# Part of the first feed-forward product by seven products of quarters in place of eight, and new planner prices for TensorE

## Chip, core and metric

One core of a Trainium2 chip runs the whole program in one launch. The metric is the device time of that launch in microseconds (us); lower is better.

## What is computed

Two layers of an encoder on 512 tokens of 1024 features. Each layer has a mixing half (one combined projection, a causal pooling mixer, sparse attention with an indexer, an output projection) and a feed-forward half. The change touches the feed-forward half alone:

```python
h = rms_norm(x, g_pre_ffn[l])
f = jnp.square(jax.nn.relu(h @ w_ff1[l])) @ w_ff2[l]
x = x + rms_norm(f, g_post_ffn[l])
```

`w_ff1` is 1024 x 4096 and `w_ff2` 4096 x 1024, all in float32.

## The kernel before

**Three passes.** TensorE works on float32r, which holds fewer digits than float32. So each float32 operand is split into a high part (a rounded copy) and a low part (operand minus high part), and each product is three matmuls: high x high, high x low, low x high (`PASSES`, line 700; `mm3`, line 702).

**Weights.** `WeightStream` (line 385) brings all weights in the order of their use. A load of 256 rows x 512 columns lands in one of two raw buffers (`wraw`); `_split` (line 445) turns each 128 rows of it into a chunk `ws` of two parts, one `copy` (high) and one `tt` subtraction (low). Eight chunks can be held (`NWS`, line 36): chunk n+8 can be split only when the last matmul on chunk n is done.

**Feed-forward.** `h`, transposed and split, lies in `A` (128 x 2 parts x 8 row blocks x 512 tokens), written by `pre_norm` (line 662) for one tile of 128 tokens at a time. The first product is made in eight blocks of 512 columns. Block 0 runs in two halves of 256 tokens, so that it can start when two token tiles are normed (banks `pf`). Blocks 1 to 7 run on all 512 tokens: 8 row blocks x 4 column tiles x 3 passes = 96 matmuls of 128 x 512, into four PSUM banks `pg`. `evac_f` (line 996) takes each bank through ReLU, square and the split into parts (tiles `fr`, then `f1h`/`f1l` or `f`). After two blocks comes their share of the second product (`ff2`): two halves of 8 chunks, 96 matmuls of 512 each, added to `facc`. Two blocks with their `ff2` are called a group here; there are four groups in a layer.

**Order.** `Planner` (line 82) records all instructions and issues them in the order of a list schedule, from a price for each instruction (`cost`, line 356) and from dependencies. What several engines can do, it assigns itself: `tt` is VectorE or GpSimd, `copy` is ScalarE or VectorE. Every engine then executes its own list in order. Since all instructions are issued from one helper, the profile puts them all on line 349; they are told apart by tile names.

Of the kernel before, what the change touches and what calls it, by code (L numbers as in the profile page):

```python
# [38 lines left out]
OUT_ORDER = (0, 1, 2, 3, 4, 5, 6, 7)  # L39
REPLACED = -3.0e38  # L40
# [41 lines left out]
class Planner:  # L82
    """Takes the instructions down in program order, finds what each depends on from the tiles that it
    reads and writes, and issues them in the order of a list schedule over the engines: of the
    instructions that an engine could start, the one with the longest chain of work behind it."""
# [141 lines left out]
    def sweep(self, key, pred, succ, late, fixed=None):  # L227
        """A list schedule. With ``fixed``, the ways are given and time runs backward."""
# [107 lines left out]
class _Recorder:  # L336
# [19 lines left out]
    def cost(self, method, args, kw, out, reads):  # L356
# [8 lines left out]
        if self.name == "pe":  # L365
            if method == "transpose":
                return 56 if args[1].dtype == F32R else 109
            return max(n / 2.4 + 2.5, 107 if free(args[1]) > 64 else 56)
# [16 lines left out]
class WeightStream:  # L385
    """Chunks of weights in the order of their use: loaded, split into two float32r parts, and held
    in a ring until their last use."""

    def __init__(self, copy, tt, sp, raw_pool, ws_pool):
        self.copy, self.tt, self.sp = copy, tt, sp  # L390
        self.raw_pool, self.ws_pool = raw_pool, ws_pool
# [4 lines left out]
        self.raw = {}  # L396

# [11 lines left out]
    def add_paired(self, src, r0, nrows, c0, ncols):  # L409
        """Chunks of 256 rows: rows r and r + 128 side by side."""  # L410
        ids = []
        for r in range(r0, r0 + nrows, 4 * P):
            k = len(self.loads)
            self.loads.append((src, r, -2, c0, ncols))
            for j in range(2):
                ids.append(len(self.chunks))
                self.chunks.append((k, j, 2 * ncols))
        return ids
# [8 lines left out]

    def _load(self):
        if self.n_load >= len(self.loads):
            return  # L430
        src, r, n, c0, ncols = self.loads[self.n_load]
        t = self.raw_pool.tile([P, 2, WMAX], F32, name="wraw")
# [12 lines left out]
    def _split(self):  # L445
# [6 lines left out]
        raw = self.raw[k][:, j, :n]  # L452
        w = self.ws_pool.tile([P, 2, WMAX], F32R, name="ws")
        self.tiles.append(w)
        self.n_split += 1
        self.copy(w[:, 0, :n], raw)
        self.tt(w[:, 1, :n], raw, w[:, 0, :n].bitcast(F32), OP.subtract)
        if j == abs(self.loads[k][2]) - 1:
            self._load()
# [10 lines left out]
def hymba_trunk(ctx: ExitStack, tc: tile.TileContext, x, positions, g_pre_mix, w_in, w_pool,  # L470
# [23 lines left out]
    wkp = ring("wkp", 1)  # L494
    tiny = ring("tiny", 4)
# [11 lines left out]
    def t2(name):  # L507
        return t2p.tile([P, WMAX], F32, name=name, tag="t2")
# [22 lines left out]
    def tt(out, a, b, op, first="dve"):  # L531
        """an elementwise instruction on SBUF, on VectorE or GpSimd"""
# [12 lines left out]
    ws = WeightStream(copy, tt, sp, rawp, wsp)  # L545
    plan = []
    for l in range(DEPTH):
# [14 lines left out]
        for g in range(4):  # L562
            for b in (2 * g, 2 * g + 1):
                p["ff1", b] = ws.add(w_ff1[l], 0, D, 512 * b, 512)
# [21 lines left out]
    identf = cst.tile([P, P], F32, name="identf")  # L586
    make_identity(nc, identf)
    ident = cst.tile([P, P], F32R, name="ident")
    dve.tensor_copy(ident, identf)
# [72 lines left out]
    def pre_norm(t, gain):  # L662
        """A[:, :, :, tile t] = the two parts of (RMSNorm(x[t]) * gain) transposed."""
# [10 lines left out]
        for hf in range(2):  # L674
# [3 lines left out]
            for j in range(4):  # L678
# [30 lines left out]
    def rope(row, t, heads):  # L709
        """in place on the first 16 of each head's 64 columns."""  # L710
# [8 lines left out]
    def heads_stacked(dst_hl, row, heads):  # L719
        """dst[128, heads, 2, 64]: the two parts of each head side by side."""  # L720
# [4 lines left out]
    def heads_doubled(dst, row, heads):  # L725
        """dst[128, 2, heads, 2, 64]: either part of each head, twice side by side."""
# [4 lines left out]
    def transposed(dst, srcs):  # L731
        """dst [128, n, 128] <- transposes of n blocks of [128, 128] in float32r."""
# [14 lines left out]
    for l in range(DEPTH):  # L747
# [4 lines left out]
        wp = cst.tile([P, 2, 4, P], F32R, name=f"wp{l}", tag="wp")  # L752
        wpr = t2("wpr")[:, :512]
        sp.dma_start(wpr.rearrange("p (g n) -> p g n", g=4), w_pool[l].rearrange("g p n -> p g n"))
        act.activation(wp[:, 0], wpr.rearrange("p (g n) -> p g n", g=4), AF.Copy)
        pool.tensor_tensor(wp[:, 1], wpr.rearrange("p (g n) -> p g n", g=4), wp[:, 0].bitcast(F32),
                           op=OP.subtract)

        # indexer projection, logits and scores
        work, iqS = {}, {}  # L760
        score = {}
        for t in range(NT):
# [26 lines left out]
            acc = wkp.tile([P, n], F32, name=f"sc{t}", tag=f"sc{t}")  # L789
# [16 lines left out]
        def select(t):  # L806
            n = P * (t + 1)
            acc = score[t]
            b = wkp.tile([P, n], F32, name=f"bias{t}", tag=f"bias{t}")
            bias[t] = b  # L810
            if n > TOPK:
                m8 = small(8, f"m8{t}")
# [50 lines left out]
        # attention  # L863
# [48 lines left out]
        def pooling_mixer():  # L912
# [12 lines left out]
            for g in POOL_PAIRS[0] + POOL_PAIRS[1]:  # L925
# [18 lines left out]
                mm3(ps, lambda a: wp[:, a, g, :], lambda b: dh[:, b], True, True)  # L944
# [6 lines left out]
        load_gain(("pre_ffn", l), g_pre_ffn, l)  # L951

        def out_pair(pair):
# [12 lines left out]
            for i, t in enumerate(tt):  # L966
                post_norm(t, banks[i], gains["post_mix", l])
                pre_norm(t, gains["pre_ffn", l])
# [13 lines left out]
        # feed-forward  # L982
        facc = None
        for g in range(4):
            f1 = []
            for bi in range(2):
# [41 lines left out]
            for hf in range(2):  # L1028
# [20 lines left out]
                for t in range(NT):  # L1049
                    if g == 0:  # L1050
                        copy(facc[:, t, cs], banks[t])
                    else:
                        dve.tensor_tensor(facc[:, t, cs], banks[t], facc[:, t, cs], op=OP.add)
        for t in range(NT):
# [30 lines left out]
```

## Time and profile before

| what | value |
|---|---|
| median of 3 runs | 1223.35 us (1222.4 to 1226.63) |
| profiled execution, first to last instruction | 1222.7 us |
| TensorE (PE) busy | 1178.5 us, 96% |
| VectorE (DVE) busy | 777.1 us, 64% |
| GpSimd (POOL) busy | 668.5 us, 55% |
| ScalarE (ACT) busy | 358.5 us, 29% |
| granted TensorE clock, mean | 0.996 of 2.4 GHz |

The page gives no other time for the profiled execution than its span, which lies inside the range of the runs. Busy time counts an instruction from its start to its end, and includes what it waits for inside. The kernel moves 115 MB through its queues, 94 GB/s in the mean.

### The profile page before, as it was taken

How to read it: one execution, taken by the hardware profiler on the slowest of the kernel's cores; microseconds unless marked ns; L12 is line 12 of the kernel's file. 1: busy time of each engine (PE TensorE's matmuls, PEld its weight loads, DVE VectorE, ACT ScalarE, POOL GpSimd, SP SyncE). 2: the span in 40 equal slices, each digit the busy share in tenths (PEclk: the TensorE clock that was granted, in tenths of full speed). 3: DMA queues.
4: the chain of work that ended last, by engine and by line, in shares of the span. 5: the costliest groups of instructions: out<-in, count | busy, mean ns of one | idle time of the engine just before them, and what ended most of it. 6: DMA issues, size and time to landing. Idle time of an engine off the chain costs nothing.

```text
span 1222.7 us, 16265 instructions
## 1 busy us (share of the span) xinstructions
PE 1178.5 (96%) x5880; PEld 978.3 (80%) x5880; DVE 777.1 (64%) x1620; ACT 358.5 (29%) x840; POOL 668.5 (55%) x628
## 2 busy tenths in 40 slices
PE   5999999999999999999989999999999999999996
PEld 5987878788888888888887878787888888888885
DVE  8899999875216335245779999998632353343344
ACT  5444677540010000000354367675201000000011
POOL 4145331358659659558334543314785695684782
PEclk9999999999999999999999999999999999999999
DMA  7222222433332322332322222234234223323221
GB/s 242 70 56 67 69 69 88 138 105 121 106 101 69 121 86 71 119 93 90 113 70 69 69 69 69 71 104 138 86 104 121 87 83 107 104 86 104 87 87 69
DMA packets 62160, 115.41 MB, mean 94 GB/s; under 512 B 5248, under 2 KB 10368, under 8 KB 62080
## 3 DMA queue, kind: packets, MB, share of 16 engines
q1 hardware_dynamic: 62080, 114.38, 29.9%
q8 instruction: 46, 0.75, 0.3%
q14 instruction: 34, 0.28, 0.1%
HBM read 112.27 MB, written 2.10 MB: 94 GB/s over the span
## 4 chain that ended last, share of the span: by engine, by line
PE 68%; DVE 23%; issue 5%; POOL 1%; DMA 1%; ACT 0%; DVEq 0%; SPq 0%; POOLq 0%; ACTq 0%
PE pg L349 58%; DVE ws L349 4%; DVE bias L349 3%; PE pi L349 2%; DVE m L349 2%; PE pf L349 2%; DVE mx L349 2%; DVE sc L349 2%; DVE x L349 1%; DVE s L349 1%; DVE A L349 1%; DVE h L349 1%; DVE pT L349 1%; PE lg L349 1%; PE pool L349 1%
## 5 line engine op out<-in xcount | busy, mean ns | idle before, releaser
L349 POOL TENSOR_TENSOR ws<-wraw,ws 128x512 fp32r<-128x512 f32 x296 | 397.6, 1350 | 278.0 <-DVE ws L349 233.3
L349 DVE CAST ws<-wraw 128x512 fp32r<-128x512 f32 (+1 forms) x317 | 195.3, 624 | 337.1 <-PE pg L349 247.4
L349 PE MATMUL pg<-A,ws 128*128 128x512 f32 x1344 | 313.9, 395 | 0.0
L349 PEld LDWEIGHTS pg<-A,ws 128*128 128x128 f32 x1344 | 252.3, 188 | 60.0
L349 PE MATMUL pg<-ws,A 128*128 128x512 f32 x864 | 226.3, 400 | 1.9 <-DVE pn L349 1.6
L349 PE MATMUL pg<-ws,f 128*128 128x512 f32 x768 | 187.0, 394 | 0.0
L349 PEld LDWEIGHTS pg<-ws,A 128*128 128x128 f32 x864 | 156.9, 188 | 33.5 <-DVE pn L349 2.5
L349 PEld LDWEIGHTS pg<-ws,f 128*128 128x128 f32 x768 | 144.1, 188 | 33.6
L349 ACT ACTIVATE fr<-pg 128x512 f32<-128x512 f32 x49 | 27.9, 598 | 475.9 <-PE pg L349 475.1
L349 PE MATMUL pg<-ws,f1h 128*128 128x512 f32 x512 | 149.5, 394 | 0.0
L349 PEld LDWEIGHTS pg<-ws,f1h 128*128 128x128 f32 x512 | 96.1, 188 | 22.5
L349 POOL TENSOR_TENSOR rstd<-rstd,neg_half 128x1 f32<-128x1 f32 x32 | 25.9, 809 | 119.5 <-DVE rstd L349 114.9
L349 PE MATMUL pg<-ws,f1l 128*128 128x512 f32 x256 | 89.1, 393 | 0.0
L349 DVE TENSOR_TENSOR ws<-wraw,ws 128x512 fp32r<-128x512 f32 (+1 forms) x104 | 79.0, 772 | 0.9 <-ACT ws L349 0.5
L349 POOL TENSOR_TENSOR fr<-fr 128x512 f32<-128x512 f32 (+1 forms) x70 | 71.3, 1033 | 12.8 <-ACT fr L349 11.8
L349 ACT ACTIVATE s<-s,st 128x384 f32<-128x384 f32 (+3 forms) x96 | 54.0, 568 | 36.0 <-DVE st L349 32.5
L349 PE MATMUL pi<-ws,A 128*128 128x292 f32 x384 | 60.7, 305 | 2.2 <-DVE ws L349 1.8
L349 ACT ACTIVATE ws<-wraw 128x512 fp32r<-128x512 f32 (+1 forms) x83 | 51.9, 632 | 30.1 <-PE pg L349 19.8
L349 PE MATMUL pool<-A,ws 128*128 128x512 f32 x192 | 58.7, 407 | 0.0
L349 PEld LDWEIGHTS pg<-ws,f1l 128*128 128x128 f32 x256 | 48.1, 188 | 11.2
L349 PEld LDWEIGHTS pi<-ws,A 128*128 128x128 f32 x384 | 53.4, 190 | 3.7 <-DVE ws L349 2.4
L349 DVE CAST f1h<-fr 128x512 fp32r<-128x512 f32 (+1 forms) x40 | 39.2, 997 | 19.0 <-POOL fr L349 19.0
(154 smaller groups left out, 1493.7 us busy)
## 6 DMA issues: line engine op xcount, KB each, us to landing
wraw<-in_w_ff_dram SPq DMA_DIRECT2D x128, 512.0 KB, 3.7
wraw<-in_w_out_dram SPq DMA_DIRECT2D x32, 512.0 KB, 3.6
wraw<-in_w_in_dram SPq DMA_DIRECT2D x24, 512.0 KB, 3.6
wraw<-in_w_in_dram SPq DMA_DIRECT2D x8, 584.0 KB, 4.1
wraw<-in_w_in_dram SPq DMA_DIRECT2D x16, 256.0 KB, 3.0
x<-in_x_dram SPq DMA_DIRECT2D x4, 512.0 KB, 6.3
out_dram<-x SPq DMA_DIRECT2D x8, 256.0 KB, 2.0
gain<-in_g_pre_mix_dram SPq DMA_DIRECT2D x2, 512.0 KB, 4.7
```

What stands on the lines that cost most here:

```text
L349: lambda: getattr(self.real, method)(*args, **kw))
```

## The change

Blocks 1 to 7 of the first product are made by a scheme of seven products. `h` (its transpose) and the 1024 x 512 weights of a block are cut into quarters: two halves of the 1024 rows, two halves of the columns, two halves of the tokens. Each of the seven products is one combination of weight quarters (names `11`, `12`, `S2`, `S1`, `S3`, `S4`, `22`) with one combination of token quarters (from `A`, or the new `T1` to `T4`): 4 row blocks x 2 column tiles x 3 passes = 24 matmuls of 128 x 256. So a block is 7 x 24 = 168 matmuls of 256 columns.

Of a block's weights, each load of 4 row blocks ("unit", tile `uraw`, 1 MB in two DMAs) is made into 7 chunks instead of 4, each split into two parts as before; four additions per unit, partly in place, make the combinations (`usum` holds one). The two units of a block lie in the two buffers `t8`, so that a unit of the next block is loaded only after the last chunk (`22`) of the same half of this one is split. `T1` to `T4` are made once per layer from an unsplit copy `hraw` of `h`. Three of the seven results are kept in SBUF (`p1`, `u2`, `p5`) and three evacuations begin with an addition.

TensorE's price goes from n / 2.4 + 2.5 to n / 2.25 + 4.5 ns for n columns. To make room, several tiles share buffers with others; block 0, the second product and the mixing half compute what they did.

```diff
-            return max(n / 2.4 + 2.5, 107 if free(args[1]) > 64 else 56)
+            return max(4.5 + n / 2.25, 111 if free(args[1]) > 64 else 60)
...
+    COMBINATIONS = ("11", "12", "S2", "S1", "S3", "S4", "22")
...
+    def add_unit(self, src, r0, c0):
...
+        for cp in range(2):
+            self.loads.append((src, r0 + 2 * cp * P, "unit", c0, 512))
+        ids = {}
+        for name in self.COMBINATIONS:
+            ids[name] = []
+            for cp in range(2):
+                ids[name].append(len(self.chunks))
+                self.chunks.append((k + cp, name, 512))
...
+        if name in ("11", "12"):
+            halves(quarter(0, int(name[1]) - 1))
+        elif name == "S2":
+            s1 = v(self.sum_pool.tile([P, 512], F32, name="usum", tag="usum"))
+            self.sums[k] = s1
+            self.tt(s1, quarter(1, 0), quarter(1, 1), OP.add)
+            self.tt(quarter(1, 0), quarter(0, 0), quarter(1, 0), OP.subtract)
+            self.tt(quarter(0, 0), s1, quarter(0, 0), OP.subtract)
+            self.tt(quarter(0, 1), quarter(0, 1), quarter(0, 0), OP.subtract)
+            halves(quarter(0, 0))
...
+            if raw is not None:
+                copy(raw[:, hf, 1 - t // 2, :, (t % 2) * P:(t % 2 + 1) * P], pv)
...
+        tt(total["T1"], hraw[:, 0, 1], hraw[:, 0, 0], OP.subtract)
...
+        for name in ("T2", "T1", "T3", "T4"):
+            copy(T[name][0], total[name])
+            tt(T[name][1], total[name], T[name][0].bitcast(F32), OP.subtract)
...
+            def product(bank, name, other, new=False):
+                for cp in range(2):
+                    w = ws.get(ids[name][cp])
+                    for j in range(2):
+                        for c in range(2):
+                            for i, (a, b) in enumerate(PASSES):
+                                pe.matmul(bank[:, 256 * j:256 * j + 256],
+                                          w[:, a, 256 * c + P * j:256 * c + P * j + P],
+                                          T[other][b][:, 2 * cp + c],
...
+            product(one, "11", "11", True)
+            p1 = kept(one, "p1")
+            product(two, "12", "21", True)
+            evac(0, LATER, two, p1)
+            product(one, "S2", "T2")
+            u2 = kept(one, "u2")
+            two = pg("two")
+            product(two, "S1", "T1", True)
+            p5 = kept(two, "p5")
+            product(one, "S3", "T3")
+            evac(1, SOONER, one, p5)
+            product(two, "S4", "22")
+            evac(0, SOONER, two, u2)
+            product(one, "22", "T4")
+            evac(1, LATER, one)
...
-                    banks = [pg() for _ in range(4)]
-                    for kc in range(KC):
-                        w = ws.get(ids[kc])
-                        for j in range(4):
-                            mm3(banks[j], lambda a: w[:, a, j * P:(j + 1) * P], lambda b: A[:, b, kc, :],
-                                kc == 0, kc == KC - 1)
-                        ws.done()
-                    for j in range(4):
-                        evac_f(j, banks[j], slice(0, S))
+                    unit_products(ids, f)
```

How the planner now orders two engines in the second group of the first layer (blocks 2 and 3). GpSimd before, from the subtractions that make the low parts of weight chunks (`ws`), some of them of blocks 2 and 3, on to the first evacuations of block 2 (`fr` squares, `f1l` low parts):

```order
L349 TENSOR_TENSOR ws<-wraw,ws 128x512 x23
L349 TENSOR_TENSOR fr<-fr 128x512 x2
L349 TENSOR_TENSOR ws<-wraw,ws 128x512
L349 TENSOR_TENSOR f1l<-fr,f1h 128x512
L349 TENSOR_TENSOR ws<-wraw,ws 128x512
```

GpSimd now, at the same place (`usum` and `uraw` as outputs are the additions that make the combinations):

```order
L350 TENSOR_TENSOR usum<-uraw 128x512 x2
L350 TENSOR_TENSOR uraw<-uraw 128x2x256
L350 TENSOR_TENSOR ws<-wraw,ws 128x512
L350 TENSOR_TENSOR uraw<-uraw 128x2x256
L350 TENSOR_TENSOR ws<-wraw,ws 128x512 x2
L350 TENSOR_TENSOR ws<-uraw,ws 128x512
L350 TENSOR_TENSOR uraw<-usum,uraw 128x2x256
L350 TENSOR_TENSOR ws<-uraw,ws 128x512
L350 TENSOR_TENSOR uraw<-usum,uraw 128x2x256
L350 TENSOR_TENSOR ws<-uraw,ws 128x512
```

The additions stand between the subtractions, which were alone here before. From the first chunk of block 2 to the first of block 4, GpSimd's list now has 57 rows: 49 tensor-tensor instructions on 512 elements and 8 squares.

VectorE now, in blocks 2 and 3, around the place where block 3's weights replace block 2's (`fr<-two,p` and `fr<-one,p` are additions that read PSUM):

```order
L350 TENSOR_TENSOR fr<-one,p_805 128x512
L350 TENSOR_SCALAR fr<-fr 128x512
L350 TENSOR_TENSOR uraw<-uraw 128x2x256
L350 CAST ws<-uraw 128x512
L350 TENSOR_TENSOR uraw<-usum,uraw 128x2x256
L350 CAST ws<-uraw 128x512
L350 TENSOR_TENSOR usum<-uraw 128x512
L350 CAST ws<-uraw 128x512 x2
L350 TENSOR_TENSOR uraw<-uraw 128x2x256
L350 TENSOR_TENSOR ws<-uraw,ws 128x512
L350 TENSOR_TENSOR uraw<-usum,uraw 128x2x256
```

VectorE now makes part of the additions and subtractions too. From the first chunk of block 2 to the first of block 4 its list has 87 rows: 50 casts, 19 tensor-tensor instructions on SBUF operands alone, 6 ReLUs on SBUF and 12 instructions that read PSUM. ScalarE's has 10 rows in the same stretch, 8 of them on PSUM.

## Rows read from the trace of the kernel before

**Rows 1.** The page: busy time, share of the span and instructions of each engine.
```profile
PE 1178.5 (96%) x5880; PEld 978.3 (80%) x5880; DVE 777.1 (64%) x1620; ACT 358.5 (29%) x840; POOL 668.5 (55%) x628
```
**Rows 2.** The chain that ended last, in order of time: start us, us, what.
```profile
265.26 5.67 PE pf L349 x48
270.94 5.95 PE pf L349 x48
276.89 328.79 PE pg L349 x1416
...
879.53 325.66 PE pg L349 x1404
```
**Rows 3.** Windows, feed-forward of layer 1: us, busy us (x instructions) of engines, clock, DMA.
```profile
core 0: us, PE busy (x) PEld busy (x) DVE busy (x) ACT busy (x) POOL busy (x), PEclk, DMA share, GB/s
367.00:456.00 89.00, 89.00 (x386) 71.97 (x385) 37.59 (x48) 4.53 (x8) 61.58 (x49) 1.00 0.30 95
277.00:606.00 329.00, 329.00 (x1421) 266.12 (x1420) 141.62 (x198) 25.56 (x49) 224.15 (x177) 1.00 0.31 98
```
**Rows 4.** Timeline, 250 to 281 us, TensorE: start us, us, instruction, count [idle before].
```profile
265.02 11.87 PE L349 MATMUL pf<-A,ws 128*128 128x256 f32 x96
```
**Rows 5.** Instructions on tile ws, 367 to 456 us: duration ns min/median/max, first and last start.
```profile
L349 POOL TENSOR_TENSOR ws<-wraw,ws x32: 1282/1292/1480, 367.6 to 453.5; 128x512 fp32r<-128x512 f32 x32
L349 DVE CAST ws<-wraw x32: 408/429/1544, 369.2 to 455.3; 128x512 fp32r<-128x512 f32 x32
```
**Rows 6.** Timeline, 387 to 404 us, GpSimd.
```profile
393.61 2.91 POOL L349 TENSOR_TENSOR ws<-wraw,ws 128x512 fp32r<-128x512 f32 x2
396.48 1.04 POOL L349 TENSOR_TENSOR fr<-fr 128x512 f32<-128x512 f32 x1
397.48 1.29 POOL L349 TENSOR_TENSOR f<-fr,f 128x512 fp32r<-128x512 f32 x1
399.13 1.29 POOL L349 TENSOR_TENSOR f<-fr,f 128x512 fp32r<-128x512 f32 x1 [0.36 <-DVE f L349]
400.38 4.15 POOL L349 TENSOR_TENSOR ws<-wraw,ws 128x512 fp32r<-128x512 f32 x3
```
**Rows 7.** The same timeline, VectorE.
```profile
392.42 2.94 DVE L349 CAST ws<-wraw 128x512 fp32r<-128x512 f32 x2
...
400.40 2.97 DVE L349 CAST ws<-wraw 128x512 fp32r<-128x512 f32 x2 [1.35 <-DMA wraw<-in_w_ff_dram]
```
**Rows 8.** Timeline, 565 to 584 us, GpSimd and VectorE where VectorE adds or subtracts.
```profile
568.72 1.49 POOL L349 TENSOR_TENSOR fr<-fr 128x512 f32<-128x512 f32 x1
...
567.91 2.84 DVE L349 TENSOR_TENSOR fr<-fr 128x512 f32<-128x512 f32 x2
570.67 0.75 DVE L349 CAST f<-fr 128x512 fp32r<-128x512 f32 x2
571.35 0.68 DVE L349 TENSOR_TENSOR f<-fr,f 128x512 fp32r<-128x512 f32 x1
```
**Rows 9.** Timeline, 408 to 413 us, VectorE adding PSUM to SBUF while GpSimd works.
```profile
410.24 1.87 DVE L349 TENSOR_TENSOR facc<-pg,facc 128x512 f32<-128x512 f32 x3
...
410.45 1.29 POOL L349 TENSOR_TENSOR ws<-wraw,ws 128x512 fp32r<-128x512 f32 x1 [0.41 <-PE pg L349]
```
**Rows 10.** DMA issues: count, KB each, median us from issue to landing.
```profile
wraw<-in_w_ff_dram SPq DMA_DIRECT2D x128, 512.0 KB, 3.7
```
**Rows 11.** Waits of TensorE, the three longest: us in total, times, longest us.
```profile
PE hT L349 <- DVE h L349: 13.0, 4, 9.4
PE tr L349 <- DVE ihl L349: 3.6, 2, 3.0
PE po L349 <- DVE early L349: 3.5, 3, 1.9
```
**Rows 12.** Groups by form, whole span, of ScalarE's casts of weights.
```profile
L349 ACT ACTIVATE ws<-wraw 128x512 fp32r<-128x512 f32 x76 | 47.1, 627 | 28.6 <-PE pg L349 18.3 <-DMA wraw<-in_w_out_dram 8.3 <-PE pi L349 0.6
```

More of the change, by code (lines that the diff above doesn't have):

```diff
@@ L396, in __init__ @@
         self.raw = {}
+        self.sums = {}
+        self.in_use = {"raw": 0, "unit": 0}
+        self.units_allowed = False
     def add(self, src, r0, nrows, c0, ncols):
@@ L426, in start, with _ahead @@
             self._split()
+    def _ahead(self):
+        while self.n_load < len(self.loads):
+            unit = self.loads[self.n_load][2] == "unit"
+            kind = "unit" if unit else "raw"
+            if self.in_use[kind] >= (2 if unit else NRAW) or unit and not self.units_allowed:
+                return
+            self._load()
     def _load(self):
@@ L431, in _load @@
         src, r, n, c0, ncols = self.loads[self.n_load]
+        if n == "unit":
+            self.in_use["unit"] += 1
+            t = self.unit_pool.tile([P, 2048], F32, name="uraw", tag="t8").rearrange(
+                "p (k c n) -> p k c n", k=2, c=2)
+            self.raw[self.n_load] = t
+            self.n_load += 1
+            for k in range(2):
+                self.sp.dma_start(t[:, k], src[r + 4 * k * P:r + (4 * k + 2) * P, c0:c0 + ncols].rearrange(
+                    "(c p) n -> p c n", p=P))
+            return
+        self.in_use["raw"] += 1
         t = self.raw_pool.tile([P, 2, WMAX], F32, name="wraw")
@@ L455, in _split @@
         self.n_split += 1
+        if isinstance(j, str):
+            self._combine(k, j, w)
+            return
+        raw = self.raw[k][:, j, :n]
         self.copy(w[:, 0, :n], raw)
@@ L458, in _split, with _combine, quarter, v @@
         if j == abs(self.loads[k][2]) - 1:
-            self._load()
+            self.in_use["raw"] -= 1
+            self._ahead()
+    def _combine(self, k, name, w):
+        raw = self.raw[k]
+        def quarter(i, j):
+            return raw[:, j, :, 256 * i:256 * i + 256]
+        def v(ap):
+            return ap.rearrange("p (c n) -> p c n", c=2)
+        high, low = v(w[:, 0, :512]), v(w[:, 1, :512])
+        def halves(value):
+            self.copy(high, value)
+            self.tt(low, value, high.bitcast(F32), OP.subtract)
+        if name in ("11", "12"):
[8 more added lines that the diff above has]
+            halves(quarter(0, 0))
+        elif name == "S1":
+            halves(self.sums[k])
+        elif name == "S3":
+            halves(quarter(1, 0))
+        elif name == "S4":
+            halves(quarter(0, 1))
+        else:
+            halves(quarter(1, 1))
+            self.in_use["unit"] -= 1
+            self._ahead()
     def get(self, i):
@@ L563, in hymba_trunk @@
             for b in (2 * g, 2 * g + 1):
-                p["ff1", b] = ws.add(w_ff1[l], 0, D, 512 * b, 512)
+                p["ff1", b] = ws.add_unit(w_ff1[l], 0, 512 * b) if b else ws.add(w_ff1[l], 0, D, 512 * b, 512)
             for hf in range(2):
@@ L951, in hymba_trunk @@
         load_gain(("pre_ffn", l), g_pre_ffn, l)
+        hraw = c1p.tile([P, 2, 2, 4, 256], F32, name="hraw", tag="c1")
         def out_pair(pair):
@@ L967, in out_pair @@
                 post_norm(t, banks[i], gains["post_mix", l])
-                pre_norm(t, gains["pre_ffn", l])
+                pre_norm(t, gains["pre_ffn", l], hraw)
         attention(2)
@@ L980, in hymba_trunk @@
             load_gain(("pre_mix", l + 1), g_pre_mix, l + 1)
+        T = {}
+        for name, tiles in (("T2", (t4("T2h"), t4("T2l"))), ("T1", (t4("T1h"), t4("T1l"))),
+                            ("T3", (mxp.tile([P, 1024], F32R, name="T3h", tag="mx"),
+                                    mxp.tile([P, 1024], F32R, name="T3l", tag="dh"))),
+                            ("T4", (wkp.tile([P, 1024], F32R, name="T4h", tag="sc"),
+                                    wkp.tile([P, 1024], F32R, name="T4l", tag="bias")))):
+            T[name] = [x.rearrange("p (c n) -> p c n", c=4) for x in tiles]
@@ new lines, in hymba_trunk @@
+        total = {"T1": hraw[:, 0, 0], "T3": hraw[:, 0, 1], "T2": hraw[:, 1, 1], "T4": hraw[:, 1, 0]}
+        tt(total["T1"], hraw[:, 0, 1], hraw[:, 0, 0], OP.subtract)
+        tt(total["T3"], hraw[:, 1, 1], hraw[:, 0, 1], OP.subtract)
+        tt(total["T2"], hraw[:, 1, 1], total["T1"], OP.subtract)
+        tt(total["T4"], hraw[:, 1, 0], total["T2"], OP.subtract)
+        for name in ("T2", "T1", "T3", "T4"):
+            copy(T[name][0], total[name])
+            tt(T[name][1], total[name], T[name][0].bitcast(F32), OP.subtract)
@@ new lines, in hymba_trunk, with unit_products, kept, evac @@
+        LATER, SOONER = slice(256, 512), slice(0, 256)
+        for name, k, cols in (("11", 0, LATER), ("21", 1, LATER), ("22", 1, SOONER)):
+            T[name] = [A[:, a, 4 * k:4 * k + 4, cols] for a in range(2)]
+        ws.units_allowed = True
+        def unit_products(ids, f):
+            one, two = pg("one"), pg("two")
+            def product(bank, name, other, new=False):
[7 more added lines that the diff above has]
+                                          T[other][b][:, 2 * cp + c],
+                                          start=new and cp == j == c == i == 0, stop=cp == c == 1 and i == 2,
+                                          skip_group_check=True)
+                    ws.done()
+            def kept(bank, name):
+                k = t2(name)[:, :512]
+                copy(k, bank)
+                return k
+            def evac(rows, cols, value, other=None):
+                r = t2("fr")[:, :512]
+                if other is not None:
+                    dve.tensor_tensor(r, value, other, op=OP.add)
+                    value = r
+                planner.either(lambda: act.activation(r, value, AF.Relu),
+                               lambda: dve.tensor_scalar(r, value, 0.0, None, op0=OP.max))
+                tt(r, r, r, OP.mult)
+                rv = r.rearrange("p (j n) -> p j n", j=2)
+                hi = f[0][:, 2 * rows:2 * rows + 2, cols]
+                copy(hi, rv)
+                tt(f[1][:, 2 * rows:2 * rows + 2, cols], rv, hi.bitcast(F32), OP.subtract)
+            product(one, "11", "11", True)
[13 more added lines that the diff above has]
+            evac(1, LATER, one)
```

43 lines of the change are left out of this document (25 added, 18 removed).

## The prediction

> **What bounds the kernel now.** I read the busy shares first: TensorE is busy 96% of the span [rows 1]. Then the chain of waits, in order of time: in each layer's feed-forward it is one unbroken run of matmuls from block 1 on, 328.79 us for 1416 of them in the first layer [rows 2]. That is 0.2322 us for a matmul of 512 columns. The windows confirm it: from 277 to 606 us TensorE is busy all 329 us at full granted clock (2.4 GHz), and of the waits of TensorE none of the three longest lies in this stage: they are of transposes of norms and heads and of attention [rows 3, 11]. So a shorter TensorE list would shorten the stage, as long as the weights come in time. That is the second thing to read: GpSimd works 61.6 of 89 us in one group of two blocks and their second product, VectorE 37.6, ScalarE 4.5 [rows 3].
>
> VectorE's time needs a closer look. The same cast of a weight chunk takes 408 ns at best and 1544 at worst [rows 5]. The timelines of the two engines show why. Two casts run after each other in 0.75 us while GpSimd waits for an input [rows 8], but two take 2.97 us when GpSimd works without a break [rows 7]: each then ends soon after an instruction of GpSimd ends. GpSimd pays less: alone, a subtraction follows the one before after 1.25 us (399.13 to 400.38), a square after 1.00 (396.48 to 397.48); with two casts among them three subtractions take 4.15 us, 0.36 more than 3 x 1.25 + 0.04 for the last one's end [rows 6, 7]. So the two engines **take turns** at something, and a cast adds 0.18 us to GpSimd's row. An addition or subtraction of VectorE on two SBUF operands adds 0.45 us: the square beside it takes 1.49 us in place of 1.04 [rows 6, 8]. VectorE instructions that read PSUM take no turn: three in 1.87 us, with GpSimd's 1.29 us untouched beside them [rows 9]. I call this shared thing the port.
>
> **TensorE's part.** Removed: 2 layers x 7 blocks x 96 matmuls x 0.2322 us = 312.1 us. Added: 2 x 7 x 168 matmuls of 256 columns. Block 0 already has such matmuls, with a new weight load before each: 48 in 5.67 us and the next 48 in 5.95 [rows 2], 0.118 and 0.124 us each, and the run of 96 in 11.87 us with its last matmul's tail lies there too [rows 4]. I take 0.120, since the slower half also waits for a few chunks: 282.2 us. **Gain 29.9 us**; ends 34.6 and 20.5.
>
> **The port's part, blocks 2 to 7.** A group before had 16 + 16 chunks; now 28 + 16, 16 additions of weights, and evacuations with additions. The lists of the two engines, from block 2's first chunk to block 4's, give the port's work in one group: GpSimd 49 x 1.25 + 8 squares x 1.00 = 69.3 us; VectorE's 50 casts and 6 ReLUs on SBUF x 0.18 = 10.1, its 19 additions and subtractions x 0.45 = 8.6. **Sum 87.9 us.** TensorE's own time for the group is now 336 x 0.120 + 192 x 0.2322 = 84.9 us, and was 384 x 0.2322 = 89.2. So the port becomes the longer of the two. Before, its work was some 61.6 us of GpSimd, waits included, in 89, with up to eight chunks of 2.8 us of TensorE each in store; now a chunk of a block lasts TensorE 12 x 0.120 = 1.4 us, as long as one cast and one subtraction take at the port (1.43).
>
> 87.9 us would need a port that never idles. VectorE has 75 instructions at the port against GpSimd's 57; the 18 without a partner cost about 0.2 us more than counted (a cast alone 0.36 against 0.18): 3.6. Its 12 PSUM instructions at 0.62 us [rows 9] stand ahead of others in its list: 7.5 us, beside GpSimd's work as long as it has some; I take 1.5 in the open. The new unit lands 3.7 us after its issue [rows 10], which cannot be before the last split of the unit that it replaces; GpSimd has about four instructions of work left then, 5 us, so nothing is added. That makes 93 us a group, 8.1 more than TensorE needs; ends 87.9 (3.0 more) and 99, with all 7.5 in the open (14.1 more). Each layer has three such groups: **49 us lost**, ends 18 and 85. ScalarE could take casts at 0.627 us [rows 12], but its list has 2 of 52 in this group.
>
> **Block 1 and the passage to it.** Block 0 holds all eight chunks to its end, so block 1's 14 are split almost as they are used. Between the first and the last of these splits stand, for the first layer, 10 GpSimd instructions (12.5 us) and 35 of VectorE at the port, with parts of `T1`, `T3` and `T4`, 10.9 us by the prices above, scaled by size: 23.4 us. 25 are without a partner, another 5. TensorE's list has 192 matmuls of 256 columns from the last use of block 0's first chunk to the first use of block 1's last: 23.0 us. Lost: 5.4 us. The eight copies of `h` to `hraw` per layer add 0.6 us each to VectorE or ScalarE in a passage where TensorE waits for norms [rows 11]; I take 1.5 us on the path. Both layers: **14 us**, ends 1 (23.4 against 23.0, copies hidden) and 30 (twice the losses).
>
> The new price of TensorE only moves the order; where TensorE waited before (13.0 us for `h`, the largest) it can win or lose some us, which the ends cover.
>
> **Sum.** 1222.7 (the span of the profiled execution, 0.65 below the median of the runs) - 29.9 + 49 + 14 = 1255.8; I say **1256 us**. The ends: 1222.7 - 34.6 + 18 + 1 = 1207, and 1222.7 - 20.5 + 85 + 30 = 1317.
>
> **Rivals.**
>
> *The store holds (faster).* All losses vanish, if the port's work in a group is below TensorE's 84.9 us: it is only 3 us above, so a cast's turn of 0.13 us in place of 0.18 would do. For it: 329 us without a wait of TensorE, though casts took up to 1544 ns [rows 3, 5]. Against it: the planner prices each engine's list as if the other were not there, and it filled GpSimd's to 69.3 of 84.9 us. The time is 1222.7 - 29.9 + 3 for block 1 = 1196.
>
> *Only the change of units costs (no change).* The port keeps up, but at the passage from block 2 to 3, 4 to 5 and 6 to 7 both buffers are full, and TensorE runs through its store while the next unit lands. Price: 3.7 us [rows 10] and one split of 0.8 us, six times, 27 us: 1222.7 - 29.9 + 27 = 1220. Against it: GpSimd's 5 us of other work at that place.
>
> *Each turn lasts its whole instruction (much slower).* Then a cast costs the port 0.41 us and a subtraction of VectorE 0.68, GpSimd's 1.29 and 1.04: 49 x 1.29 + 8 x 1.04 + 56 x 0.41 + 19 x 0.68 = 107.4 us a group, 22.5 over TensorE, six times 135; block 1 and the passage lose some 10 in each layer, 21. 1222.7 - 29.9 + 156 = 1349. Against it: with a cast in every turn GpSimd's row still advances by 1.43 us, not by 1.70 [rows 6, 7]. This is the rule of the Trainium skill, SBUF — State Buffer, "SBUF: two separate sides": the port pair that VectorE and GpSimd share is an exclusive lock, held for the whole instruction, while the other is blocked. The rows here agree that one waits for the other, and for which instructions, but not with the length.
>
> That TensorE does not run 24 matmuls of 256 columns for a product is excluded by its list, which has 168 for a block.
>
> **Chances.** Forecast 0.63, the store holds 0.20, only the units 0.10, whole turns 0.07. Under 0.3% (3.7 us) is about what a measurement of this kernel cannot tell from no change. Faster: 0.20, some 0.04 of the units' case and the forecast's lowest end, 0.01: 0.25. Same: 0.10, from the units' case and the forecast's low end. Slower: 0.65. The range, 1194 to 1305 us, takes in a little over half of the first rival's chance and stops short of the forecast's upper end; out of it lie 0.08 of the first rival, 0.07 of the last and 0.03 of the forecast. The forecast's own range is 1207 to 1317.
>
> **What would show it.** Right: TensorE's matmuls of 256 columns at 0.118 to 0.124 us in unbroken runs, but with waits in blocks 1 to 7 whose releaser is VectorE's or GpSimd's `ws`; VectorE and GpSimd together without a gap there, GpSimd's subtractions near 1.45 us and casts over 1 us in the mean; a group near 93 us in the windows, ScalarE under 15% busy. Wrong: groups near 85 us with TensorE at 100% (the store holds); waits that end with a DMA of `uraw` (the units); GpSimd's row at 1.7 us (whole turns); or the time lost elsewhere, in the passages or the mixing half.

## The result and the profile after

The changed kernel takes **1366.45 us** (median of 4 runs, 1362.66 to 1370.93) against 1223.99 us (1222.4 to 1226.63) for the kernel before: ratio 1.1163, 95% interval 1.1134 to 1.1191. The forecast, 1256 us, had the direction; but its size was far too small, and its range ended at 1305. The profiled execution spans 1360.9 us, 138.2 more than before.

The page of the changed kernel, busy times, clock by slices and shares of the chain, answers to [rows 1, 2]:

```profile
span 1360.9 us, 18672 instructions
PE 1197.8 (88%) x6888; PEld 1036.2 (76%) x6888; DVE 1101.6 (81%) x1924; ACT 362.8 (27%) x839; POOL 848.3 (62%) x729
PEclk8999999988997998998999999999899989889988
DVE 47%; PE 35%; issue 7%; POOL 5%; DMA 5%; ACT 2%; DVEq 0%; SPq 0%; POOLq 0%; ACTq 0%
```

Clock and chain of the page before:

```profile
PEclk9999999999999999999999999999999999999999
PE 68%; DVE 23%; issue 5%; POOL 1%; DMA 1%; ACT 0%; DVEq 0%; SPq 0%; POOLq 0%; ACTq 0%
```

TensorE is no longer most of the chain: nearly half of it is VectorE. TensorE's busy time has even risen, though by the forecast 29.9 us of matmuls are gone; the clock row says why a busy time can rise.

Where the time lies is read from stage to stage. The stages begin with TensorE's first matmul into `pf` (block 0) and the first of each second product; times in us:

| stage | before | after | forecast of the change | measured |
|---|---|---|---|---|
| mixing half, layer 1 | 249.0 | 269.8 | 0 | +20.8 |
| blocks 0 and 1, layer 1 | 50.1 | 68.3 | +4.9 | +18.2 |
| three groups, layer 1 | 267.5 | 299.2 | +11.7 | +31.7 |
| last second product, layer 1 | 45.3 | 47.0 | 0 | +1.7 |
| mixing half, layer 2 | 240.4 | 255.0 | 0 | +14.6 |
| feed-forward, layer 2 | 361.2 | 411.6 | +16.5 | +50.4 |

(A group counts here from one second product to the next, so that the forecast's 29.9 us of gain are 4.3 in each of six groups and 2.1 in each block 1. The last 9.2 and 10.0 us, after TensorE's last matmul, are not in the table.) The windows of the changed kernel, the first over the mixing half, the others over blocks 2 to 5 and their second products (columns as in [rows 3]):

```profile
0.00:269.80 269.80, 237.63 (x1293) 197.92 (x1294) 238.15 (x596) 134.61 (x326) 116.44 (x152) 0.98 0.30 92
...
387.60:438.10 50.50, 39.72 (x295) 38.40 (x294) 47.26 (x55) 5.30 (x9) 37.44 (x28) 0.86 0.29 96
438.10:487.30 49.20, 49.20 (x233) 40.54 (x232) 27.54 (x33) 1.72 (x3) 40.88 (x30) 1.00 0.23 73
487.30:538.10 50.80, 39.88 (x298) 38.01 (x297) 46.33 (x58) 6.01 (x10) 35.53 (x27) 0.90 0.29 97
538.10:587.70 49.60, 49.60 (x236) 40.91 (x235) 25.16 (x28) 2.35 (x4) 42.32 (x33) 1.00 0.22 71
```

A group takes 99.7 us (50.50 + 49.20), and falls into two halves. In the first, where the seven products run (I call it the unit stretch), TensorE has gaps and a lower granted clock, and VectorE is full. In the second, the 192 matmuls of a second product and some 40 of the next block's, TensorE has no gap, and VectorE works half of the time. The waits of TensorE over the whole span, three longest:

```profile
PE one L350 <- DVE fr L350: 43.9, 12, 6.5
PE one L350 <- DVE ws L350: 29.8, 21, 6.0
PE hT L350 <- ACT h L350: 11.3, 2, 9.3
```

The second of them, chunks that come late, I had foreseen. The first I had not: products into the bank `one` that wait for an evacuation. TensorE's timeline in the first group shows one, and what it leaves behind:

```profile
405.14 1.71 PE L350 MATMUL one<-A,ws 128*128 128x256 f32 x13
406.68 1.70 PE L350 MATMUL two<-A,ws 128*128 128x256 f32 x13
...
413.59 1.05 PE L350 MATMUL two<-A,ws 128*128 128x256 f32 x4
...
432.92 0.80 PE L350 MATMUL one<-T4h,ws 128*128 128x256 f32 x2 [6.16 <-DVE fr L350]
```

At 405 us 13 matmuls take 1.54 us to the next row, 0.118 each, as forecast. At 413.59, after two gaps of over a us, four take 1.05 us with a step of 0.21: the granted clock is at its lower level, 1.2 GHz (0.50 from 413.6 to 414.6 us). At 432.92 TensorE has waited 6.16 us for VectorE. VectorE's timeline before that, and GpSimd's:

```profile
422.10 0.68 DVE L350 TENSOR_TENSOR fr<-two,p 128x512 f32<-128x512 f32 x1
422.70 3.78 DVE L350 CAST ws<-uraw 128x512 fp32r<-128x512 f32 x3
426.40 1.75 DVE L350 TENSOR_TENSOR ws<-uraw,ws 128x512 fp32r<-128x512 f32 x1
428.08 0.41 DVE L350 CAST ws<-wraw 128x512 fp32r<-128x512 f32 x1
428.41 0.68 DVE L350 TENSOR_TENSOR ws<-uraw,ws 128x512 fp32r<-128x512 f32 x1
429.01 1.48 DVE L350 CAST ws<-wraw 128x512 fp32r<-128x512 f32 x1
430.42 0.41 DVE L350 TENSOR_SCALAR fr<-fr 128x512 f32<-128x512 f32 x1
430.75 1.51 DVE L350 CAST ws<-wraw 128x512 fp32r<-128x512 f32 x1
432.19 0.68 DVE L350 TENSOR_TENSOR fr<-one,p 128x512 f32<-128x512 f32 x1
```

```profile
423.29 1.47 POOL L350 TENSOR_TENSOR f1l<-fr,f1h 128x512 fp32r<-128x512 f32 x1
424.73 1.47 POOL L350 TENSOR_TENSOR ws<-uraw,ws 128x512 fp32r<-128x512 f32 x1
426.16 1.45 POOL L350 TENSOR_TENSOR f1l<-fr,f1h 128x512 fp32r<-128x512 f32 x1
428.57 1.64 POOL L350 TENSOR_TENSOR ws<-wraw,ws 128x512 fp32r<-128x512 f32 x1 [0.97 <-DVE ws L350]
430.57 1.41 POOL L350 TENSOR_TENSOR ws<-wraw,ws 128x512 fp32r<-128x512 f32 x1 [0.36 <-DVE ws L350]
```

The addition that frees the bank (`fr<-one,p`) takes 0.68 us and reads PSUM, so it has no turn to wait for. But it stands in VectorE's list behind casts and a subtraction that wait for GpSimd (1.26 to 1.51 us in place of 0.41, and 1.75 in place of 0.68). GpSimd in turn idles 0.97 and 0.36 us for VectorE's casts. The turns themselves are as priced: with a cast in each, GpSimd's row advances by 1.44 and 1.43 us; beside a subtraction of VectorE and the start of a cast its instruction takes 1.64.

### The profile page after: what moved, and what is told of

It is laid out like the page before. It is cut to its first block, busy times and chain, and to the rows that moved or that the text cites. A ratio compares the mean times of both kernels' runs of the same rounds, so it can differ in the third digit from the quotient of the medians.

```text
span 1360.9 us, 18672 instructions
## 1 busy us (share of the span) xinstructions
PE 1197.8 (88%) x6888; PEld 1036.2 (76%) x6888; DVE 1101.6 (81%) x1924; ACT 362.8 (27%) x839; POOL 848.3 (62%) x729
## 4 chain that ended last, share of the span: by engine, by line
DVE 47%; PE 35%; issue 7%; POOL 5%; DMA 5%; ACT 2%; DVEq 0%; SPq 0%; POOLq 0%; ACTq 0%
PE pg L350 22%; DVE ws L350 16%; PE one L350 4%; DVE bias L350 4%; DVE fr L350 3%; DVE m L350 3%; PE pi L350 2%; POOL ws L350 2%; DMA uraw<-in_w_ff_dram 2%; PE two L350 2%; DVE s L350 2%; DMA wraw<-in_w_ff_dram 2%; DVE A L350 2%; DVE uraw L350 2%; DVE f1h L350 1%
## 5 line engine op out<-in xcount | busy, mean ns | idle before, releaser
L350 POOL TENSOR_TENSOR ws<-wraw,ws 128x512 fp32r<-128x512 f32 (+1 forms) x211 | 291.5, 1389 | 172.4 <-DVE ws L350 92.1
L350 POOL TENSOR_TENSOR ws<-uraw,ws 128x512 fp32r<-128x512 f32 x97 | 138.6, 1433 | 71.3 <-DVE ws L350 59.4
L350 DVE CAST ws<-uraw 128x512 fp32r<-128x512 f32 x143 | 117.4, 836 | 55.7 <-PE pg L350 43.6
L350 PE MATMUL two<-A,ws 128*128 128x256 f32 x672 | 110.7, 292 | 7.5 <-DVE ws L350 4.3
L350 PEld LDWEIGHTS two<-A,ws 128*128 128x128 f32 x672 | 97.9, 199 | 11.5 <-DVE ws L350 4.5
L350 PE MATMUL one<-T4h,ws 128*128 128x256 f32 x224 | 56.2, 335 | 43.9 <-DVE fr L350 43.9
L350 PE MATMUL one<-A,ws 128*128 128x256 f32 x336 | 61.2, 298 | 17.0 <-DVE ws L350 17.0
L350 DVE TENSOR_TENSOR ws<-uraw,ws 128x512 fp32r<-128x512 f32 x71 | 71.1, 1008 | 0.2
L350 PEld LDWEIGHTS one<-A,ws 128*128 128x128 f32 x336 | 53.3, 203 | 22.0 <-DVE ws L350 19.1
L350 POOL TENSOR_TENSOR uraw<-uraw 128x512 f32<-128x512 f32 x43 | 61.6, 1437 | 13.0 <-DVE uraw L350 6.6
```

The lines of the kernel that those rows point to most:

```text
L350: lambda: getattr(self.real, method)(*args, **kw))
```

## The experiments

All times are medians; ratios are to the kernel before, with their 95% intervals. Three theories stood: the **port** (VectorE and GpSimd taking turns), the **price** (TensorE's new price in the planner), and **VectorE's list** (too many instructions there, port or not).

### The price alone, out of and into a kernel

`e1_old_price` is the changed kernel, `e2_before_new_price` the kernel before, each with the other's prices. There are two of them: the change also raised the price of a transpose in float32r from 56 to 59 ns. In e1:

```diff
-                return 59 if args[1].dtype == F32R else 109
-            return max(4.5 + n / 2.25, 111 if free(args[1]) > 64 else 60)
+                return 56 if args[1].dtype == F32R else 109
+            return max(n / 2.4 + 2.5, 107 if free(args[1]) > 64 else 56)
```

> The changed kernel with TensorE's old price (n / 2.4 + 2.5), nothing else undone. The mixing half took some 35 us more in the changed kernel than before. If the new price caused that by another order, the time falls to 1325 to 1340 us; if the shared buffers or the copies of h did, it stays at 1355 to 1375 us.

> The kernel before with the new price of TensorE alone. If the price makes the mixing half slower, 1245 to 1260 us; if it does nothing, 1218 to 1230 us.

Measured: e1 1297.5 us, 1.061 (1.0568 to 1.0652); e2 1273.69 us, 1.0415 (1.0385 to 1.0445). Both miss their ranges: the prices cost more than either expectation had. So **69 us of the changed kernel's time go with these two prices**, and the same prices cost the kernel before 50 us. In e2 the mixing halves take 272.0 and 258.5 us (+23 and +18), its groups 89 to 90 as before. In e1 they take 255.9 and 240.5, 6.9 and 0.1 more than before, so the shared buffers and the copies of `h` cost little.

The three groups of e1's layer 1 take 91.3, 93.1 and 95.5 us (from the main run of one second product to the next), near the forecast's 93; those of layer 2 take 97.2, 97.7 and 101.5. The window of the second group of layer 1:

```profile
406.90:500.00 93.10, 87.08 (x530) 76.99 (x529) 72.08 (x97) 19.32 (x33) 39.64 (x28) 0.98 0.28 92
```

GpSimd has 28 instructions here, against 28 + 30 in the group of the changed kernel shown above. By the prices of the prediction these lists put only 61 to 70 us on the port in each group of layer 1, less than TensorE's 84.9, so the sum would have forecast no loss. That these groups come near 93 is chance.

### The port

`e3_no_pool_ff` takes GpSimd out of the conversions of the feed-forward weights, the combinations and the evacuations of blocks 1 to 7: VectorE does its work there. `e4_act_casts` gives the casts of these weights to ScalarE instead, and leaves the subtractions free.

Of e3, and then of e4 (not shown: both also mark the loads of these weights):

```diff
+    def tt_ff(out, a, b, op):
+        dve.tensor_tensor(out, a, b, op=op)
...
+    ws.ff_tt = tt_ff
...
-                tt(r, r, r, OP.mult)
+                tt_ff(r, r, r, OP.mult)
```

```diff
+    ws.ff_copy = lambda out, a: act.activation(out, a, AF.Copy)
```

> The changed kernel with all additions, subtractions and squares of the feed-forward's weights and of blocks 1 to 7 on VectorE, none on GpSimd. Port theory (VectorE and GpSimd wait for each other): VectorE alone has 76 x 0.65 + 56 x 0.36 + 12 x 0.65 = 77 us of work in a group, below TensorE's 85, so a group falls from 100 to 86 to 92 us and the time to 1270 to 1320 us. Theory that VectorE's list in order is the limit (TensorE's longest waits end with VectorE's additions that free a bank): the list gets longer, a group stays at 100 us or more and the time at 1360 us or more.

> The changed kernel with the casts of the feed-forward's weights on ScalarE, GpSimd's work as it was. Port theory: 44 casts of a group leave the port, 8 us, and it then has about 80 us of work in a group: 91 to 95 us a group, 1305 to 1340 us in all. Theory of VectorE's list: 44 casts at 0.8 us leave it, 35 us, so the waits go and a group takes 86 us, 1270 to 1290 us in all.

Measured: e3 1273.26 us, 1.0412 (1.0381 to 1.0442); e4 1319.78 us, 1.0792 (1.0761 to 1.0823). One group of each, in windows; e3 in three pieces, e4 in two:

```profile
387.50:424.30 36.80, 36.80 (x312) 36.76 (x311) 35.95 (x69) 9.66 (x17) 0.00 (x0) 1.00 0.28 92
424.30:463.40 39.10, 39.10 (x171) 31.58 (x171) 31.12 (x60) 0.60 (x1) 0.00 (x0) 1.00 0.40 130
463.40:471.50 8.10, 8.10 (x49) 7.11 (x48) 6.20 (x12) 0.00 (x0) 0.00 (x0) 1.00 0.00 0
```

```profile
427.00:476.00 49.00, 49.00 (x233) 40.59 (x232) 9.61 (x13) 13.71 (x23) 42.07 (x34) 1.00 0.27 87
476.00:521.20 45.20, 38.35 (x300) 37.50 (x299) 36.13 (x37) 15.73 (x27) 35.13 (x25) 0.92 0.31 102
```

One engine fewer, and the group falls from 99.7 to 84.0 us, with TensorE at 100% throughout. In the unit stretch VectorE executes 69 instructions in 36 us, where 55 filled 47 beside GpSimd's 28 (ScalarE takes 17 in place of 9). VectorE's list is longer and the group shorter, which ends the theory of VectorE's list. e4, with the casts off the port, stands at 94.2, between the two, as the port theory had it.

e3 takes away the hand-overs between the two engines together with the turns. The lengths of VectorE's instructions part the two. In the unit stretch of the changed kernel its 33 instructions with one SBUF input and its 15 with two take 46.5 us in sum; at 0.41 and 0.68 us, their lengths beside an idle GpSimd, it would be 23.7. Its seven on PSUM keep to 0.68. So the turns lengthen VectorE's list by 22.7 us there, while it idles 1.2 us for GpSimd. In e3 the casts and subtractions of units are near their short lengths again, here over its whole span:

```profile
L350 DVE TENSOR_TENSOR ws<-uraw,ws 128x512 fp32r<-128x512 f32 x168 | 119.7, 727 | 2.4 <-ACT ws L350 1.0
L350 DVE CAST ws<-uraw 128x512 fp32r<-128x512 f32 x110 | 47.8, 444 | 30.5 <-PE pg L350 26.7
```

### Both, and a version near the kernel before

`e5_no_pool_old_price` joins e3 and the old price.

> The changed kernel with GpSimd out of blocks 1 to 7 and of the feed-forward's weights, and with TensorE's old price. If the two causes found so far add up (GpSimd out: 93 us, price: 51 to 69 us), 1205 to 1225 us; if the price's cost goes another way once the feed-forward's lists change, 1240 to 1275 us.

Measured: 1223.08 us, 0.999 (0.9978 to 1.0002). The feed-forward halves gain 9.2 and 10.0 us (353.7 and 351.2), the mixing halves lose 10.6 and 7.8. In blocks 0 and 1 it still takes 55.8 us (50.1 before). So `e6_block1_whole` made block 1 as before, with the seven products from block 2 on, and `e9_block1_whole_act_casts` added e4's casts. Of e6, without the loop that makes block 1:

```diff
-                p["ff1", b] = ws.add_unit(w_ff1[l], 0, 512 * b) if b else ws.add(w_ff1[l], 0, D, 512 * b, 512, True)
+                p["ff1", b] = ws.add_unit(w_ff1[l], 0, 512 * b) if b > 1 else ws.add(w_ff1[l], 0, D, 512 * b, 512, True)
```

> The same, with block 1 made whole as before (seven products from block 2 on). With GpSimd out of the feed-forward, block 0 and block 1 still took some 13 us per layer more than before, because all chunks of block 1 are split almost as they are used. If that is the reason, 15 to 25 us less than the kernel with block 1 by seven products, at 1185 to 1210 us; if T1 to T4 and the copies of h are, 0 to 8 us less.

> Block 1 whole, GpSimd out, old price, and the casts of the feed-forward's weights on ScalarE too. VectorE then has 76 x 0.65 + 12 x 0.65 + 12 x 0.36 = 62 us in a group in place of 77, ScalarE 35. If VectorE still holds TensorE up anywhere in the feed-forward, 5 to 15 us less than without; if not, within 4 us of it or, by another order of the mixing half, to either side.

Measured: 1231.82 us, 1.0063 (1.004 to 1.0086), and 1235.41 us, 1.0097 (1.0067 to 1.0126). e6 is a miss: blocks 0 and 1 came to 53.9 us, 1.9 less than in e5, and the first chunks of block 2 and the waits for the evacuation of block 1 (`pg` for `fr`, 14.7 us in two) took that and more. e9 lies within 4 us of e6, which was expected if VectorE no longer holds TensorE up in the feed-forward.

### How far an order is a draw

The planner starts from a little noise, set by `SEED`. Changing it alone redraws the order: `e7_before_seed54` in the kernel before, `e10_new_price_seed54` in e2, `e11_after_seed54` in the changed kernel, `e12_no_pool_old_price_seed5` and `e13_no_pool_old_price_seed19` in e5.

```diff
-    SEED = 53
+    SEED = 54
```

> The kernel before with the seed of the planner's noise at 54 in place of 53, prices as they were. If the new price of TensorE is bad in itself, 1218 to 1230 us. If any other order of the mixing half is late by tens of us and the one of before is a lucky draw, 1240 to 1290 us.

> The kernel before with the new price of TensorE, and SEED 54 in place of 53. If the new price is a worse price in itself, every order drawn with it is longer: about 1265 to 1285 us, as with seed 53 (1273.7 us). If the price only gave another draw, and the order of the kernel before is a favourable draw, the time falls among the draws: about 1235 to 1255 us, near the 1243.0 us that SEED 54 gave at the old price. The feed-forward halves stay at 360 to 363 us in both; what differs is the mixing halves.

> The changed kernel with SEED 54 in place of 53. If the loss of the changed kernel comes from what runs on GpSimd and VectorE (the port) and from the price, a new draw changes little: 1345 to 1385 us, groups of the feed-forward half still 97 to 102 us. If this order was an unlucky draw: 1310 to 1340 us, groups near 93 us.

> The changed kernel with the old price, without GpSimd in the feed-forward half, and SEED 5 in place of 53. With SEED 53 this gave 1223.1 us: 19 us won in the two feed-forward halves, 18 us lost in the mixing halves. If the mixing halves' loss is that of a draw, another draw should give some of it back: 1200 to 1220 us. If the pieces in the feed-forward half force it, 1220 us and above. The feed-forward halves stay at 350 to 355 us in both.

> The same with SEED 19. If the mixing halves' loss is that of a draw: 1200 to 1220 us; if the pieces in the feed-forward half force it, 1220 us and above.

| kernel | SEED 53 | another seed |
|---|---|---|
| before | 1224 | 1243.02, 1.0159 (1.0118 to 1.02) |
| before, new price | 1273.7 | 1269.98, 1.0372 (1.0354 to 1.0391) |
| changed | 1366.45 | 1371.53, 1.1207 (1.1188 to 1.1226) |
| e5 | 1223.1 | 1229.17, 1.0043 (1.0027 to 1.006), and 1218.04, 0.9955 (0.9938 to 0.9972) |

A draw moves the time by some 4 to 19 us. By its expectation, e7's 1243 us spoke for a lucky draw of the kernel before; but the new price costs 27 us or more above either order of it, which two seeds at each price make unlikely to be a draw alone. **The last is faster than both kernels**, by 0.45%, the best of three seeds: its feed-forward halves take 353.7 and 355.1 us, its mixing halves 253.5 and 246.6, still 4.5 and 6.2 more than before.

### Does the price act through engines or through the order?

The price of TensorE sets the due times by which the planner gives a conversion to one engine or another (`sooner`, which compares an engine's end with `late`). The instructions on `ws` in the first mixing half, on ScalarE and GpSimd, show that it chose otherwise (durations ns min/median/max). Of the kernel before, from 0 to 249 us:

```profile
L349 ACT ACTIVATE ws<-wraw x39: 612/632/692, 8.9 to 245.7; 128x512 fp32r<-128x512 f32 x36, 128x584 fp32r<-128x584 f32 x3
L349 POOL TENSOR_TENSOR ws<-wraw,ws x29: 1263/1298/3634, 51.7 to 224.0; 128x512 fp32r<-128x512 f32 x29
```

Of e2, which differs in the price alone, from 0 to 272 us:

```profile
L349 POOL TENSOR_TENSOR ws<-wraw,ws x54: 1261/1295/1752, 43.3 to 246.3; 128x512 fp32r<-128x512 f32 x54
L349 ACT ACTIVATE ws<-wraw x14: 613/632/685, 11.2 to 269.3; 128x512 fp32r<-128x512 f32 x10, 128x584 fp32r<-128x584 f32 x4
```

25 casts move from ScalarE to VectorE, and 25 subtractions from VectorE to GpSimd, onto the port on both sides, in the half in which VectorE is busy 230.81 of 249.00 us:

```profile
0.00:249.00 249.00, 230.59 (x1292) 193.84 (x1293) 230.81 (x593) 144.87 (x349) 85.87 (x130) 1.00 0.32 100
```

The changed kernel shows the same over its whole span: with the new price GpSimd has 729 instructions and ScalarE 839, with the old one (e1) 599 and 981.

To part the choice of engines from the order, the kernel before was planned twice: once to choose, then, engines fixed, to order, with either price at either step (0 is old, 1 new). f0 is the control, and f3 does f1's edit on the changed kernel. The heart of f1's edit:

```diff
+        self.ops = self.priced(kept, 0)
+        _, way = self.plan()
+        self.ops = self.priced([([ways[w]], deps, soft) for (ways, deps, soft), w in zip(kept, way)], 1)
+        start, _ = self.plan()
```

> The kernel before, planned twice: first to choose the engine of each instruction that has a choice, then, with those engines fixed, to set the order; the old price of TensorE in both. It is the control of the next two: the second planning draws a new order, so 1223 to 1245 us, the band of the two seeds at the old price. ScalarE keeps about 39 and 37 tile casts in the two mixing halves, as in the kernel before.

> Engines chosen with the old price, order set with the new one. If the new price costs time through the choice of engines (at the new price ScalarE casts 14 and 14 tiles of the mixing halves in place of 39 and 37, and GpSimd subtracts 54 and 54 in place of 29 and 33, beside a VectorE that is busy throughout), the time comes back: 1223 to 1250 us. If it costs time through the order: 1262 to 1280 us, as the two seeds with the new price alone gave.

> The reverse: engines chosen with the new price, order set with the old one. Choice of engines: 1258 to 1280 us. Order: 1223 to 1250 us.

> The changed kernel, engines chosen with the old price, order set with the new one. The changed kernel took 1366 us, with the old price in both 1297.5 us. Choice of engines: 1285 to 1320 us, and ScalarE at some 430 us busy. Order: 1345 to 1380 us.

Measured: f0 1232.68 us, 1.0065 (1.0045 to 1.0084); f1 1257.29, 1.0272 (1.0252 to 1.0292); f2 1252.5, 1.0232 (1.0212 to 1.0252); f3 1343.04, 1.0964 (1.0942 to 1.0986). f1, f2 and f3 each fall between their two ranges, so neither theory holds alone: against the control the engines cost 20 us and the order 25, and both together 37 to 41. f3 parts the 69 us of the changed kernel in the same way: 23 go with the engines (1366.45 to 1343.04), 46 with the order. Each of these runs is one order, though, and a draw alone moves the time by 4 to 19 us; the shares are rough.

## Why the prediction was wrong

**TensorE's part: right.** 0.118 us for a matmul of 256 columns; where nothing else binds (e3), the group shown takes 84.0 us and the six take 84.8 in the mean, against 84.9 forecast. The gain is there, and it is covered.

**The port's part: the turns as priced, the sum over a group the wrong measure.** The step that failed is the comparison of the port's "Sum 87.9 us" with TensorE's 84.9 for a whole group: it averages over the group. The groups by form in the unit stretch, 387.60 to 438.10 us (count, busy us, mean ns, idle before), GpSimd:

```profile
L350 POOL TENSOR_TENSOR ws<-uraw,ws 128x512 fp32r<-128x512 f32 x10 | 14.3, 1438 | 5.9 <-DVE ws L350 3.1 <-ACT ws L350 1.9 <-PE two L350 0.4
L350 POOL TENSOR_TENSOR fr<-fr 128x512 f32<-128x512 f32 x7 | 8.7, 1241 | 3.4 <-DVE fr L350 3.4
L350 POOL TENSOR_TENSOR ws<-wraw,ws 128x512 fp32r<-128x512 f32 x4 | 5.8, 1446 | 1.7 <-DVE ws L350 1.7
```

and VectorE:

```profile
L350 DVE CAST ws<-uraw 128x512 fp32r<-128x512 f32 x15 | 16.3, 1107 | 2.5 <-PE pg L350 2.2 <-DMA uraw<-in_w_ff_dram 0.3
L350 DVE TENSOR_TENSOR ws<-uraw,ws 128x512 fp32r<-128x512 f32 x7 | 8.9, 1265 | 0.0
```

By the prices of the prediction, GpSimd's 28 instructions there (7 of them squares) cost 21 x 1.25 + 7 x 1.00 = 33.3 us of the port, VectorE's 33 with one SBUF input 5.9 and its 15 with two 6.8; its other 7 read or copy PSUM. That is **46 us, where TensorE needs 34.8** (its 295 matmuls there, at the rate of e3's window, 312 in 36.80 us). The same count for 438.10 to 487.30 us gives 41.6, where TensorE needs all of the 49.2. The sum, 88, is the 87.9 of the prediction; but the second half's slack is no use to the first, and TensorE is late by 11.2 us, not 3, even with a perfect port. The port is not perfect: 50.5 us for 46, 4.5 more (forecast 5.1), since GpSimd's idle time ends mostly with VectorE's part of the same chunk. 11.2 + 4.5 makes 15.7 us a group, all of it in the unit stretch, where the forecast had 8.1 for the group.

Seen from TensorE, these 15.7 us are 10.8 of gaps and 4.9 of longer busy time (39.72 us for 34.8): 33 steps at the lower granted clock, 3.1 us, and the tails of matmuls ahead of the gaps.

The sum has a second fault. It counts the port, while VectorE also has its own work to do, and its list with the waits for turns is what is full: 47.26 of 50.50 us in this stretch. In e1, from 459.26 to 500.00 us, the port's work by the same prices is 31.5 us and TensorE's 34.5, yet the stretch takes 40.7, with VectorE busy 38.20 of it. What binds there was not tested by itself.

Why the work is not done ahead, in the slack, is argued only: a chunk can be split only when its place among eight is free, and the second half of a unit lands while the stretch already runs. Its transfer lies on the chain once in each of six groups, 3.6 to 5.6 us each, 27 in all, though TensorE never waits for it. So the rival of the units had its place right; that e3 with the same transfers is bound by TensorE says that it decides nothing alone. A longer ring was not tried.

**Block 1 and the passage: 7 us lost per layer in the forecast, 20 and 17 measured** (18.2 and 14.8 more than before, and 2.1 of gain). VectorE has no slack there (busy 36.85 of 37.80 and 29.53 of 30.50 us in the windows of layer 1's passage). But GpSimd taken out of the weights gives back little: 63.8 us of 68.3 are left in layer 1 and 62.4 of 64.2 in layer 2 (e3). The old price alone leaves 59.7 and 60.6 (e1), both together 55.8 and 53.5 (e5). So the port is at most a part of this loss, more of layer 1's goes with the price, and the rest is not parted.

**The new price: the step that was plainly wrong, and the largest.** The prediction says that it "only moves the order" and "can win or lose some us, which the ends cover": it cost 69 us (e1), 28 in the mixing halves, 27 and 10 in the feed-forward halves of the two layers. Of the 105 us by which the profiled execution exceeds the forecast (138.2 more than before in place of 33.1), 67 go with it (1360.9 against 1293.7). I had read the price as a matter of TensorE, and TensorE has no choice of engine. The planner, though, counts back from TensorE's list when each conversion is due, and chooses its engine by that. With the old price the changed kernel would have come to 1297.5, inside the range given, and in part by chance: the port's sum, taken from e1's lists, is too small for the groups of its layer 1. What the new price does to the order itself, beyond the engines (25 us in f1), stays open; in f1's mixing half TensorE's busy time grew too, at a granted clock of 0.96.

**The rivals.** Whole turns had 1349 us, nearest to the result, and for the wrong reason. The Trainium skill, SBUF — State Buffer, "SBUF: two separate sides", states a lock for the whole instruction; by that rule a cast would move GpSimd's row on to 1.66 us (1.25 + 0.41), if the 1.25 us hold the port throughout. The trace after shows 1.43 to 1.44, as that of before did, and disagrees with the length. "The store holds" (1196) asked for less port work than TensorE's. That is the case with GpSimd out, where TensorE does run without a gap in the group shown, but blocks 0 and 1 and the mixing halves keep most of the gain. It is also the case in layer 1 of e1, and there the losses did not vanish.

## What to carry to other kernels

When two engines share a port, compare its work with the time of the bound engine stretch by stretch, between the points where the store is empty, not over a whole period; a store evens out only what it can hold. Count too what the turns add to the list of the engine that waits for them, for that list has other work behind it. A price in a planner is an edit to every choice that hangs on it, on all engines: list which instructions changed their engine before pricing anything else. And in a kernel with a drawn order, measure a second seed before believing a difference of 1 or 2 per cent.

## What the runs showed of the hardware

Two engines were slower than one: without GpSimd a unit stretch took 36.8 us (e3: VectorE 69 instructions, ScalarE 17), while with it the stretch took 50.5 us (VectorE 55, GpSimd 28, ScalarE 9). A subtraction on 128 x 512 elements takes a step of 1.25 us on GpSimd and 0.68 us on VectorE, each alone. Beside a GpSimd that works without a break a cast of VectorE takes 1.5 us in place of 0.41, and GpSimd's step grows by 0.18. The granted clock of TensorE fell in the unit stretches of the changed kernel to means of 0.86 to 0.90, and after gaps of 1 to 6 us matmuls of 256 columns followed each other at 0.21 us (granted clock 0.50 from 413.6 to 414.6 us) in place of 0.118; in the stretches without a gap it is 1.00.
